# Fixed tiles of a twelve-phase transformer kernel placed at multiples of 512 bytes

## The chip, the cores and the metric

The kernel runs on 1 core of one Trainium2 chip. The metric is the device time of one execution in microseconds (us), lower being better. TensorE multiplies matrices into PSUM, VectorE (DVE) and ScalarE (ACT) do elementwise work, and the queue of SyncE (SP) issues the transfers between HBM and SBUF. SBUF has 128 partitions; an address below is the byte offset inside a partition, the same in all 128.

## The reference, cut to what matters

The input is 256 tokens of width 1024 in float32. Two blocks follow each other, each twice (depth 2). The first block is conditioned: a vector c gives shift, scale and gate for each of three steps (feed-forward, a mixer of four groups, feed-forward). The second has three steps of the same kind with plain gains and norms on both sides.

```python
for l in range(DEPTH):                       # first block
    sh1, sc1, g1, ... = split(silu(c) @ ada_w[l] + ada_b[l], 9)
    hn = modulate(rms_norm(h, g), sh1, sc1)
    h = h + 0.5 * g1 * swiglu(hn, ffn1_w_in[l], ffn1_w_out[l])      # 1024 -> 2 x 2816 -> 1024
    z = modulate(rms_norm(h, g), sh2, sc2) @ w_in[l]                # attention, convolution, gMLP, forgetting attention
    h = h + g2 * (concat(o_a, o_b, o_c, o_d) @ w_out[l])
    h = h + 0.5 * g3 * swiglu(modulate(rms_norm(h, g), sh3, sc3), ffn2_w_in[l], ffn2_w_out[l])
for l in range(DEPTH):                       # second block
    x = x + 0.5 * rms_norm(swiglu(rms_norm(x), ...))
    x = x + rms_norm(merged(hgrn2, sliding attention) @ w_out[l])
    x = x + 0.5 * rms_norm(swiglu(rms_norm(x), ...))
```

All of it is float32. The weights of the large products, 692 tiles of 512 KB in the packing of the kernel, are read once.

## The kernel before, in words

There are twelve phases, 0 to 11: three per layer, two layers per block, two blocks. Phases 0, 2, 3, 5, 6, 8, 9 and 11 are feed-forwards, phases 1 and 4 mixers of the first block, 7 and 10 of the second. By the trace of before, phase 0 ends at about 228 us, phase 2 runs from about 372 to 565, phase 3 from there to 763, the first block ends at about 1084 and phase 8 begins at about 1478.

The activations of a norm lie transposed in two fixed tiles, xh and xl, [128 features, 8 x 256 tokens]: the value rounded to the tensor engine's float32r, and the rest. A weight tile [128, 1024] is loaded raw (wr, 3 buffers), ScalarE casts it to wh (9 buffers; L321) and VectorE subtracts to get wl (9 buffers; L322). A large product is three passes, in `mm3` at L346 to L349:

```python
T.matmul(acc, a, wh, start=start, stop=False)     # L347: high part times high part
T.matmul(acc, a, wl, start=False, stop=False)     # L348
T.matmul(acc, b, wh, start=False, stop=stop)      # L349: low part
```

The first operand behind the accumulator, [128, 128], is stationary and is loaded before each pass; the second, [128, 512], moves. In the trace a product is written with the moving operand first (`a<-wh,xh`).

Two loops call it. `gemm_cols` and `gemm_pair` (a "column product") take xh and xl as stationary operands and hold two accumulators per chunk of 512 columns, one for each half of the tokens. `gemm_rows` (a "row product") takes the stationary operands from scratch slots: gh and gl of a hidden chunk, made by `split` into slots of the s2 pool (22 buffers of 2048 bytes, names s in the trace), and goes round four accumulators. The two are never mixed: a column product's stationary operand is always xh or xl, a row product's always a slot. Two small products have operands elsewhere: L1101 moves lev_h over lf, and the gate column of the first block (L347 with `t<-xh,wf`) moves xh over 4 columns of wf.

The order on each engine comes from a scheduler that follows the program's order by priority; weights are called for two keys ahead (AHEAD), and the modulation columns of the first block (ada, 144 tiles of 512 KB, L628) are loaded and multiplied on VectorE between the pieces of phases 0 to 5, spread by PACE0, PACEM and PACE1.

Where the tiles lie is set by the order in which the pools' tiles are made. The fixed tiles (pool const) come first, from byte 16512 of each partition, in the order h, col_sb, identb, xh, xl, epsc, mod, an (sizes 8192, 3520, 256, 8192, 8192, 8, 288 twice, 96 twice, each rounded up to 32). The pools wr, wh, wl, s2, s1, sm and row follow, then the pools of the blocks. So the bytes past a multiple of 512 were: h 128, xh and xl 320, every slot of wr, wh, wl and s2 96, lev_h 96, lf 480, wf 352 and 96, ada 224.

Of the kernel before, what the change touches and what calls it, by code (L numbers as in the profile page):

```python
# [9 lines left out]
F32 = mybir.dt.float32  # L10
F32R = mybir.dt.float32r
# [11 lines left out]
TAPS = 31  # L23
FIRST = 3  # chunks of the first product that share its k-outer loop
AHEAD = 2  # weight tiles loaded before their use
TAIL, TAIL1 = 4, 3  # last weight tiles of a product that run one token tile after the other
NORM_WAIT = 5  # pieces of a product between a norm's arithmetic and its transposes
CONV_STEP = 2  # taps of the convolution per piece
BOOST = 40  # instructions by which a norm's chain comes forward
PACE0, PACEM, PACE1 = 30.0, 3.0, 31.0  # weight tiles over which a phase spreads its modulation columns  # L30
NS2, NS1, NW, NR, NA = 22, 5, 9, 3, 2  # buffers

# [190 lines left out]
def body(ctx, tc, ws, cols, x, c, adaw, wf, gmn, wst, bmask, lev, pred, sbias, gains, lbs, out, phases=range(12)):  # L223
# [39 lines left out]
    def row_tile():  # L263
        return row_p.tile([128, D], F32, tag="row", name=nm("row"))

    h = const.tile([128, 2, D], F32, name="h")
    col_sb = const.tile([128, NCOL], F32, name="col_sb")
# [6 lines left out]
    identb = const.tile([128, 128], BF16, name="identb")  # L274
    xh = const.tile([128, 8, S], F32R, name="xh")
    xl = const.tile([128, 8, S], F32R, name="xl")
    epsc = const.tile([128, 2], F32, name="epsc")
# [3 lines left out]
    @contextmanager  # L281
    def sooner(n):
        """the instructions inside come before ones emitted up to n earlier where both are ready"""
        p0 = tc.cur_priority
        tc.cur_priority = p0 - n
        yield
        tc.cur_priority += n

# [1 line left out]
    threads = []  # L290
# [27 lines left out]

# [1 line left out]
    def split(dst_h, dst_l, src):  # L320
# [3 lines left out]
    loaded = {}  # L324
# [44 lines left out]
    def gemm_pair(key0, key1):  # L369
        """the first two chunks of a phase: token tile 0 of both, then token tile 1"""  # L370
        acc = [[accum(), accum()] for _ in range(2)]
        w = {}
        for t in range(2):
            until(lambda: t in normed)
            for n, key in enumerate((key0, key1)):
                if t == 0:
                    w[n] = [weights(key + (i,)) for i in range(2)]
                for k in range(8):
                    mm_cols(acc[n], w[n], k, t)
                    if k % 2:  # L380
                        pump()
        normed.clear()
        return acc
# [30 lines left out]

# [1 line left out]
    def rsqrt(dst, src, scale, eps=0):  # L416
        """1 / sqrt(scale * src + eps) from the tables, refined by a Newton step"""
        n = src.shape[1]
        v, a = sm(n), sm(n)
        A.activation(a, src, AF.Ln, scale=scale, bias=epsc[:, eps:eps + 1])  # L420
        A.activation(a, a, AF.Exp, scale=-0.5)
        V.tensor_scalar(out=v, in0=src, scalar1=scale, scalar2=(1.0, 4.0)[eps] * EPS, op0=ALU.mult, op1=ALU.add)
        V.tensor_tensor(out=v, in0=v, in1=a, op=ALU.mult)
        V.scalar_tensor_tensor(out=v, in0=v, scalar=-0.5, in1=a, op0=ALU.mult, op1=ALU.mult)
        V.scalar_tensor_tensor(out=dst, in0=v, scalar=1.5, in1=a, op0=ALU.add, op1=ALU.mult)
# [7 lines left out]
    def row_rstd(halves, half=False, boost=0):  # L433
        """1 / rms of rows given as two halves; half: 0.5 / rms"""
        ss = sm(2)
        for i, src in enumerate(halves):
            junk = s1([128, 512], BF16)
            A.activation(junk, src, AF.Square, accum_out=ss[:, i:i + 1])  # L438
        r = sm(1)
        with sooner(boost):  # L440
            V.tensor_tensor(out=r, in0=ss[:, 0:1], in1=ss[:, 1:2], op=ALU.add)
            rsqrt(r, r, (4.0 if half else 1.0) / D, 1 if half else 0)
        return r
# [13 lines left out]
    def deferred(ph):  # L457
        """phases whose products take rows without their 1 / rms, which then scales the results"""
        return ph >= 6 and ph % 3 != 1
# [38 lines left out]
    def boundary(ph, t, acc):  # L498
        """residual of phase ph, norm of the next one"""
        if ph < 6 and t == 0:  # L500
# [29 lines left out]

# [1 line left out]
    def ffn(ph, first=None):  # L532
# [39 lines left out]
    def to_features(src):  # L572
        """[128 tokens, 256] x 2 token tiles -> PSUM [128 features, 2, 256 tokens]"""
        ps = tp([128, 2, S])
        for t in range(2):
            for i in range(2):
                T.transpose(ps[:, i, 128 * t:128 * t + 128], src[t][:, 128 * i:128 * i + 128], ident)  # L577
        return ps
# [16 lines left out]
    def exp_rows(ps, n, nmx, sums, cols, floor=None):  # L595
        """exp(ps - row max) of n score maps into SBUF; row sums into the given columns"""
        pb = s2([128] + list(ps.shape[1:]))
        V.tensor_reduce(out=nmx, in_=ps, axis=AX.X, op=ALU.max, negate=True)
        if floor is not None:
            V.tensor_tensor(out=nmx, in0=nmx, in1=floor, op=ALU.min)  # L600
        for i in range(n):
            A.activation(pb[:, i], ps[:, i], AF.Exp, bias=nmx[:, i:i + 1], accum_out=sums[:, cols[i]:cols[i] + 1])
        return [pb[:, i] for i in range(n)]

    def keys_first(p):
        """probabilities [queries, 128 keys] of four heads, keys on partitions"""
        ps = tp([128, 4, 128])
# [5 lines left out]

# [1 line left out]
    first_block = ctx.enter_context(ExitStack())  # L615
    mod = [const.tile([128, 72], F32, name=f"mod{l}") for l in range(2)]
    an = [const.tile([128, 24], F32, name=f"an{l}") for l in range(2)]
    c1 = pool("c1", 1, first_block)
    ada_p = pool("ada", NA, first_block)
# [12 lines left out]
    def ada_finish(l, n, w):  # L632
        """bias of columns n .. n + w of one segment; scale columns also give norm_g * (1 + scale)"""
        s = slice(n, n + w)
# [32 lines left out]
    def start():  # L667
        """the first norm's modulation as its columns arrive, FIRST chunks of the first product at a time"""
        xts = [s2([128, 2, S]) for _ in range(4)]
# [72 lines left out]
    def mix1(ph):  # L742
# [13 lines left out]
        def layer_norms(srcs):  # L756
            """normalised rows of two [128 tokens, 256]"""
            mv, r, nb = sm(4), sm(2), sm(2)
# [79 lines left out]
        def qk_norms(acc, group):  # L838
            """RMS norms over groups of columns of two [128 tokens, 512]"""
            n = 512 // group  # L840
# [11 lines left out]
        def weighted(pts, v):  # L852
            """four heads' p @ v in PSUM [128 queries, 4, 64]"""
            o = tp([128, 4, 64])
# [5 lines left out]
        def diff(acc):  # L860
# [11 lines left out]
            for t in range(2):  # L872
                keys = 128 * (t + 1)
                ts = slice(128 * t, 128 * t + 128)
                sums = sm(8)
                # maps of one 32-row group of the tensor engine share a PSUM bank
                for j in range(4):
# [43 lines left out]
        def decay():  # L921
            """the running sum of -log_sigmoid(f), heads on partitions"""
            ps = tp([4, S])
# [78 lines left out]

# [1 line left out]
    def setup2():  # L1004
# [13 lines left out]
        nc.sync.dma_start(out=sb, in_=sbias.rearrange("p (a b) -> p a b", a=8))  # L1018
        # log of the softmax over the two depths: [log(1 - lb), log(lb)]
        lb = c2.tile([128, 2, 512], F32, name="lb")  # L1020
# [18 lines left out]
    def mix2(ph):  # L1039
# [20 lines left out]
        def gates(acc):  # L1060
            """log forget gates split for the tensor engine (tokens on partitions), keys (features on partitions)"""
            lb = G2["lb"]
# [27 lines left out]
        def hgrn():  # L1090
            lf, kT, qT, v, sg = got["lf"], got["k"], got["q"], got["hv"], got["sg"]
            far, sts = [], []
            for t in range(2):
# [14 lines left out]
                def weigh(b):  # L1108
                    """decays times keys on the first half of each pair of blocks, times queries on the second"""
                    for c_, src in ((0, kT[t]), (1, qT[t])):  # L1110
# [23 lines left out]
                def second(b):  # L1134
                    """columns of the second half of each pair of blocks"""
                    return lambda ap: ap.rearrange("p h (n c b) -> p h n c b", c=2, b=b)[:, :, :, 1]
# [64 lines left out]
        def swa_kv():  # L1201
            """one 256-column chunk: keys, features on partitions, and values"""
            w = weights(("b2", l, "akv"))
# [122 lines left out]

# [1 line left out]
    rest = {0: [2, 4, 3, 5, 7, 6], 2: [8, 10, 9], 3: [11, 13, 12, 14, 16, 15], 5: [17]}  # L1328
# [79 lines left out]
```

## Time and profile before

| | |
|---|---|
| median of 3 runs | 2254.09 us |
| lowest and highest | 2253.39 and 2263.06 us |
| span of the profiled execution | 2261.4 us |
| TensorE busy, granted clock | 2185.8 us (97%), 0.990 of 2.4 GHz |
| VectorE, ScalarE busy | 1493.7 us (66%), 1188.8 us (53%) |
| read from HBM | 450.03 MB, 199 GB/s over the span |
| weight tiles | 692 transfers of 512 KB, 4.1 us from issue to landing |

The profile is one execution, and its span is 7 us over the median of the runs. The span is from the first to the last instruction of the program; the runs' times also hold what lies around it, which the profile does not show. Busy shares of TensorE count overlapping instructions once, so 97% says that it hardly pauses and not how quickly it goes.

### The profile page before, as it was taken

To read this page: it belongs to the slowest core of one execution; us is meant where nothing else is said; L and a number is where in the kernel's file an instruction comes from. 1 tells how busy PE (TensorE), PEld (TensorE's weight loads), DVE (VectorE), ACT (ScalarE), POOL (GpSimd) and SP (SyncE) were. 2 spreads that over 40 slices of the span, in tenths; PEclk is the share of its full clock that TensorE was granted. 3 is DMA by queue.
4 is the path that set the end of the run, shared out by engine and by line. 5 is a ranking of instruction groups with operands and counts; after the bars stand their busy time and mean duration, and the time that the engine had idled before them with its cause. 6 is when DMAs were issued, how large, how long until landed. Compare 5 with 4: busy or idle time off the path is not lost.

```text
span 2261.4 us, 27880 instructions
## 1 busy us (share of the span) xinstructions
PE 2185.8 (97%) x10148; PEld 1766.1 (78%) x10150; DVE 1493.7 (66%) x2251; ACT 1188.8 (53%) x1914; POOL 0.2 (0%) x4
## 2 busy tenths in 40 slices
PE   5999897999999998999999999999999999999998
PEld 4877676888788776888788888878888887887887
DVE  7878885765887786654755666575565557657553
ACT  5544655544544656543654566464455447546542
POOL 0000000000000000000000000000000000000000
PEclk9999998999999999999999999999999999999999
DMA  8889633876798733665655543475556556245652
GB/s 314 305 299 323 232 104 123 286 256 216 282 322 304 240 112 112 223 200 190 220 195 184 171 159 104 139 220 184 184 180 200 183 167 199 92 142 165 203 181 93
DMA packets 125417, 452.91 MB, mean 200 GB/s; under 512 B 14176, under 2 KB 14432, under 8 KB 125280
## 3 DMA queue, kind: packets, MB, share of 16 engines
q1 hardware_dynamic: 125280, 451.13, 59.9%
q8 instruction: 80, 1.31, 0.2%
q14 instruction: 57, 0.47, 0.1%
HBM read 450.03 MB, written 1.05 MB: 199 GB/s over the span
## 4 chain that ended last, share of the span: by engine, by line
PE 73%; DMA 11%; DVE 7%; ACT 5%; issue 3%; SPq 0%; DVEq 0%; ACTq 0%
PE a L347 22%; PE a L349 21%; PE a L348 21%; DMA wr<-in_ws 9%; DVE wl L322 3%; ACT wh L321 3%; PE t L577 2%; DVE spill L628 1%; DMA ada<-in_adaw 1%; PE t L451 1%; PE t L1147 1%; PE t L1101 1%; PE t L883 1%; ACT h L438 1%; PE t L609 0%
## 5 line engine op out<-in xcount | busy, mean ns | idle before, releaser
L322 DVE TENSOR_TENSOR wl<-wr,wh 128x1024 fp32r<-128x1024 f32 x692 | 844.2, 1223 | 493.2 <-ACT wh L321 490.7
L321 ACT CAST wh<-wr 128x1024 fp32r<-128x1024 f32 x692 | 725.7, 1051 | 753.4 <-PE a L349 430.4
L347 PE MATMUL a<-wh,xh 128*128 128x512 f32 x1888 | 761.5, 404 | 20.9 <-ACT xh L686 8.3
L348 PE MATMUL a<-wl,xh 128*128 128x512 f32 x1888 | 746.9, 396 | 0.0
L349 PE MATMUL a<-wh,xl 128*128 128x512 f32 x1888 | 745.7, 396 | 0.0
L347 PEld LDWEIGHTS a<-wh,xh 128*128 128x128 f32 x1888 | 357.7, 190 | 106.6 <-ACT xh L686 10.5
L349 PEld LDWEIGHTS a<-wh,xl 128*128 128x128 f32 x1888 | 356.3, 189 | 88.5 <-DVE xl L496 2.2
L348 PEld LDWEIGHTS a<-wl,xh 128*128 128x128 f32 x1888 | 357.8, 190 | 79.3
L347 PE MATMUL a<-wh,s 128*128 128x512 f32 x896 | 352.8, 394 | 7.8 <-ACT s L321 3.9
L348 PE MATMUL a<-wl,s 128*128 128x512 f32 x896 | 351.6, 392 | 1.7 <-DVE wl L322 1.7
L349 PE MATMUL a<-wh,s 128*128 128x512 f32 x896 | 349.9, 392 | 0.3 <-DVE s L592 0.3
L347 PEld LDWEIGHTS a<-wh,s 128*128 128x128 f32 x896 | 168.8, 188 | 45.0 <-ACT s L321 5.1
L348 PEld LDWEIGHTS a<-wl,s 128*128 128x128 f32 x896 | 169.0, 189 | 36.9 <-DVE wl L322 2.8
L349 PEld LDWEIGHTS a<-wh,s 128*128 128x128 f32 x896 | 169.1, 189 | 36.1 <-DVE s L592 0.7
L628 DVE CUSTOM_DVE_ANT_0 spill<-ada,cond 128x1024 bf16<-128x1024 f32 x144 | 175.6, 1220 | 17.3 <-DMA ada<-in_adaw 16.3
L451 PE MATMUL t<-col_sb,s 128*128 128x128 f32 x304 | 46.8, 291 | 31.9 <-DVE s L474 26.3
L451 PEld LDWEIGHTS t<-col_sb,s 128*128 128x128 f32 x304 | 36.8, 148 | 45.0 <-DVE s L474 18.9
L322 DVE TENSOR_TENSOR s<-t,s 128x512 fp32r<-128x512 f32 x96 | 64.7, 683 | 1.9 <-ACT s L321 1.7
L321 ACT CAST s<-t 128x512 fp32r<-128x512 f32 x96 | 54.9, 583 | 18.6 <-PE t L577 18.6
L577 PE MATMUL t<-col_sb,h 128*128 128x128 f32 x392 | 58.3, 273 | 3.7 <-DVE h L546 2.1
L542 ACT ACTIVATE h<-a,m 128x256 f32<-128x256 f32 x88 | 40.6, 472 | 39.5 <-PE a L349 39.4
L577 PEld LDWEIGHTS t<-col_sb,h 128*128 128x128 f32 x392 | 47.8, 140 | 17.2 <-DVE h L546 3.3
(234 smaller groups left out, 1249.6 us busy)
## 6 DMA issues: line engine op xcount, KB each, us to landing
wr<-in_ws SPq DMA_DIRECT2D x692, 512.0 KB, 4.1
ada<-in_adaw SPq DMA_DIRECT2D x144, 512.0 KB, 4.8
row<-in_gains SPq DMA_DIRECT2D x12, 512.0 KB, 4.9
h<-in_x SPq DMA_DIRECT2D x2, 512.0 KB, 5.7
out<-h SPq DMA_DIRECT2D x4, 256.0 KB, 2.1
cond<-in_c SPq DMA_DIRECT2D x1, 512.0 KB, 4.2
gmn<-in_gmn SPq DMA_DIRECT2D x2, 256.0 KB, 5.3
wst<-in_wst SPq DMA_DIRECT2D x2, 256.0 KB, 6.1
```

The costliest lines, as they stand in the source:

```text
L321: A.copy(dst_h, src)
L322: V.tensor_tensor(out=dst_l, in0=src, in1=dst_h.bitcast(F32), op=ALU.subtract)
L347: T.matmul(acc, a, wh, start=start, stop=False)
L348: T.matmul(acc, a, wl, start=False, stop=False)
L349: T.matmul(acc, b, wh, start=False, stop=stop)
L438: A.activation(junk, src, AF.Square, accum_out=ss[:, i:i + 1])
L451: T.transpose(ps[:, j], src[:, 128 * j:128 * j + 128], ident)
L542: A.activation(g, acc[t][:, 0:256], AF.Silu, scale=r)
L577: T.transpose(ps[:, i, 128 * t:128 * t + 128], src[t][:, 128 * i:128 * i + 128], ident)
L628: ins = V.tensor_tensor_reduce(out=spill, in0=raw, in1=cond, scale=1.0, scalar=0.0, op0=ALU.mult, op1=ALU.add, accum_out=mod[l][:, n:n + 1])
L883: T.matmul(ps[:, i], qT[rs, i, ts], kT[rs, i, 0:keys], start=False, stop=i == 1)
L1101: T.matmul(ps.rearrange("p a b -> p (a b)"), lf[t][n][:, hs], G2["lev"][:, o:o + 512], start=n == 0, stop=n == 1)
```

## The change

The fixed tiles are made in another order: an unused tile of 384 bytes, xh, xl, h, col_sb, identb, epsc, mod, an, and an unused tile of 32 bytes. The first moves xh to byte 16896 (33 x 512), the last moves the first weight buffer to byte 46080 (90 x 512). As the slots are 4096 and 2048 bytes long, the bytes past a multiple of 512 become: h, xh and xl 0, every slot of wr, wh, wl and s2 0, lev_h 0, lf 384, wf 256 and 0, ada 128. The instructions, their order on each engine and what each waits for are those of before. The diff also drops comments and docstrings.

```diff
+    const.tile([128, 96], F32, name="lead")
+    xh = const.tile([128, 8, S], F32R, name="xh")
+    xl = const.tile([128, 8, S], F32R, name="xl")
     h = const.tile([128, 2, D], F32, name="h")
     col_sb = const.tile([128, NCOL], F32, name="col_sb")
...
     ident = C("ident")
     identb = const.tile([128, 128], BF16, name="identb")
-    xh = const.tile([128, 8, S], F32R, name="xh")
-    xl = const.tile([128, 8, S], F32R, name="xl")
     epsc = const.tile([128, 2], F32, name="epsc")
...
     mod = [const.tile([128, 72], F32, name=f"mod{l}") for l in range(2)]
     an = [const.tile([128, 24], F32, name=f"an{l}") for l in range(2)]
+    const.tile([128, 8], F32, name="trail")
     c1 = pool("c1", 1, first_block)
```

## Rows read from the trace of the kernel before

**Rows 1.** Page: busy us, share of the span; DMA share and GB/s in 40 slices.

```profile
PE 2185.8 (97%) x10148; PEld 1766.1 (78%) x10150; DVE 1493.7 (66%) x2251; ACT 1188.8 (53%) x1914; POOL 0.2 (0%) x4
...
DMA  8889633876798733665655543475556556245652
GB/s 314 305 299 323 232 104 123 286 256 216 282 322 304 240 112 112 223 200 190 220 195 184 171 159 104 139 220 184 184 180 200 183 167 199 92 142 165 203 181 93
```

**Rows 2.** Page: shares of the chain that ended last, by line.

```profile
PE a L347 22%; PE a L349 21%; PE a L348 21%; DMA wr<-in_ws 9%; DVE wl L322 3%; ACT wh L321 3%; PE t L577 2%; DVE spill L628 1%; DMA ada<-in_adaw 1%; PE t L451 1%; PE t L1147 1%; PE t L1101 1%; PE t L883 1%; ACT h L438 1%; PE t L609 0%
```

**Rows 3.** Chain by line: stretches 0-252, 252-567, 567-768, 768-2262 us, in this order.

```profile
by line: DMA wr<-in_ws 40.8%; issue 9.0%; ACT wh L321 8.8%; DVE spill L628 8.6%; DVE wl L322 8.6%; DMA ada<-in_adaw 5.8%; DMA col_sb<-in_cols 2.7%; PE a L347 2.1%; PE a L348 2.0%; PE a L349 2.0%; DVE s L322 1.2%; SPq L627 0.8%; DVE s L474 0
by line: PE a L349 23.7%; PE a L347 23.7%; PE a L348 23.5%; issue 3.2%; DVE wl L322 2.4%; PE t L883 2.2%; DMA wst<-in_wst 2.1%; PE t L857 1.7%; PE t L451 1.6%; PE t L577 1.5%; DMA wr<-in_ws 1.4%; PE t L964 1.3%; PE t L962 1.3%; ACT wh L321 
by line: DMA wr<-in_ws 20.7%; PE a L347 15.9%; PE a L349 15.9%; PE a L348 15.7%; DMA ada<-in_adaw 7.1%; ACT wh L321 5.0%; issue 4.6%; DVE wl L322 3.8%; DVE spill L628 3.8%; PE t L577 1.5%; ACT s L494 0.9%; DVE h L546 0.9%; PE t L451 0.8%; A
by line: PE a L347 25.1%; PE a L349 24.9%; PE a L348 24.9%; DMA wr<-in_ws 3.9%; PE t L577 1.9%; DVE wl L322 1.7%; ACT wh L321 1.6%; issue 1.4%; PE t L1147 1.2%; PE t L451 1.2%; PE t L1101 1.0%; ACT h L438 0.8%; PE t L1259 0.7%; PE t L1241 0
```

**Rows 4.** Busy time by stretch, in us; last three: granted clock, DMA share, GB/s.

```profile
core 0: us, PE busy (x) PEld busy (x) DVE busy (x) ACT busy (x) POOL busy (x), PEclk, DMA share, GB/s
567.00:768.00 201.00, 195.92 (x871) 157.76 (x870) 163.27 (x235) 98.72 (x141) 0.00 (x0) 0.99 0.84 298
1465.00:2262.00 797.00, 783.79 (x3672) 638.68 (x3670) 469.31 (x638) 419.63 (x656) 0.00 (x0) 1.00 0.53 170
1109.00:1115.00 6.00, 6.00 (x28) 4.81 (x27) 4.07 (x4) 2.88 (x5) 0.00 (x0) 1.00 0.81 268
1229.00:1236.00 7.00, 7.00 (x33) 5.79 (x32) 3.27 (x3) 2.81 (x3) 0.00 (x0) 1.00 0.63 205
```

**Rows 5.** Timeline of TensorE, product from xh, xl: start us, us, instruction; 22 rows.

```profile
1109.70 0.40 PE L349 MATMUL a<-wh,xl 128*128 128x512 f32 x1
...
1114.60 0.39 PE L349 MATMUL a<-wh,xl 128*128 128x512 f32 x1
```

**Rows 6.** Timeline of TensorE, product from scratch slots; 27 rows.

```profile
1229.81 0.39 PE L347 MATMUL a<-wh,s 128*128 128x512 f32 x1
...
1235.70 0.39 PE L349 MATMUL a<-wh,s 128*128 128x512 f32 x1
```

**Rows 7.** Timeline of TensorE, L1101 behind a product.

```profile
1325.13 0.39 PE L349 MATMUL a<-wh,xl 128*128 128x512 f32 x1
1325.36 2.02 PE L1101 MATMUL t<-lev_h,lf 128*128 128x512 f32 x8
```

**Rows 8.** Timeline of TensorE, the product with wf; 8 rows.

```profile
804.36 0.28 PE L347 MATMUL t<-xh,wf 128*4 128x256 f32 x1
...
805.15 0.28 PE L348 MATMUL t<-xl,wf 128*4 128x256 f32 x1
```

**Rows 9.** Groups by shape, TensorE: count, busy us, mean ns, idle before.

```profile
L347 PE MATMUL a<-wh,xh 128*128 128x512 f32 x1856 | 752.2, 406 | 20.9 <-ACT xh L686 8.3 <-ACT xh L495 7.5 <-ACT wh L321 3.0
L347 PE MATMUL a<-wh,s 128*128 128x512 f32 x896 | 352.8, 394 | 7.8 <-ACT s L321 3.9 <-ACT wh L321 3.0 <-ACT s L591 0.7
```

**Rows 10.** Timeline of TensorE, a bf16 product and what follows.

```profile
1375.03 0.38 PE L1237 MATMUL t<-sb,identb 128*128 128x512 bf16 x1
1375.24 1.05 PE L1241 MATMUL t<-h,s 128*128 128x128 f32 x8
```

**Rows 11.** Groups by shape, ScalarE and VectorE.

```profile
L321 ACT CAST s<-t 128x512 fp32r<-128x512 f32 x96 | 54.9, 583 | 18.6 <-PE t L577 18.6
L321 ACT CAST xh<-t 128x512 fp32r<-128x512 f32 x24 | 13.8, 579 | 1.0 <-PE t L451 0.7
L322 DVE TENSOR_TENSOR s<-t,s 128x512 fp32r<-128x512 f32 x96 | 64.7, 683 | 1.9 <-ACT s L321 1.7
L322 DVE TENSOR_TENSOR xl<-t,xh 128x512 fp32r<-128x512 f32 x24 | 16.1, 686 | 5.7 <-ACT xh L321 5.5
```

## The prediction

> **What bounds the kernel now.** I read the page's busy table and slices first, then the chain of waits, then both stage by stage. TensorE is busy 97% of the span, VectorE 66%, ScalarE 53% [rows 1], and the three lines of the three-pass product (L347 to L349) hold 64% of the chain [rows 2]. The stages differ. From 768 us to the end those lines hold 75% of the chain and weight transfers 4%; from 252 to 567 us it is 71% and 1.4%. From 0 to 252 us they hold 6%: the chain runs through the weight transfer, its cast, its subtraction and the modulation columns. From 567 to 768 us it is mixed, 48% products and 28% transfers [rows 3], with the queue at 298 GB/s, against 170 GB/s later [rows 4]. So a shorter product counts in all stages but phases 0 and 3.
>
> A busy TensorE may still run at different paces, and the timeline of its starts shows that it does. The durations overlap and are of no use here; the starts are. In a product from xh and xl, 22 rows from 1109.70 to 1114.60 us are 21 steps: 4.90 / 21 = 0.2333 us each [rows 5]. In a product from scratch slots, 27 rows from 1229.81 to 1235.70 us are 26 steps: 5.89 / 26 = 0.2265 us [rows 6]. Same shape, same granted clock (1.00, the 2.4 GHz level) [rows 4], same number of weight loads, no wait on either side: 6.8 ns differ.
>
> What differs is where the stationary operand lies. The moving weights (wh, wl) begin 96 bytes past a multiple of 512 in both. Scratch slots also begin at 96, xh and xl at 320. A third pair: the gates' sums (L1101) move lev_h (96) over lf (480); the eight begin at 1325.36 us and their busy stretch is 2.02 us, so with 0.39 us for the last one the seven steps are 0.233 us [rows 7]. Equal remainders go with the quick pace, unequal ones with the slow one, in another line with another operand. A fourth pair is less clear: eight 256-column products of the gate column move xh (320) over wf (352 and 96) with only 4 columns to load; 0.79 / 7 = 0.113 us, or 0.226 us for 512 columns, the quick pace [rows 8].
>
> The Trainium skill ("TensorE: Matmul & The Clock Gate", Step-by-step: what each phase is for) says that TensorE has two independent read ports and that loading the next stationary tile takes no read bandwidth from the running matmul. By that, the remainders would cost nothing and the two paces would have some other cause; the rows don't decide it, so this is the first rival below.
>
> **The change part by part.** No instruction is added, removed, reordered or given another wait; only addresses move.
>
> *xh, xl and weight slots to a common remainder.* After the change the stationary xh and xl, the scratch slots and the weights all begin at 0 past a multiple of 512, so every large product has equal remainders, as scratch-slot products have now. I take the quick pace for all: 0.2333 - 0.2265, rounded to 6.7 ns saved per product. There are 3 x 1856 = 5568 such products of 512 columns [rows 9]. By the code: 528 in each of 8 feed-forward phases (11 chunks x 8 k x 2 token tiles x 3 passes), 240 in each mixer of the first block, 432 in each mixer of the second. Where products lead the chain:
> - Feed-forward phases 2, 5, 6, 8, 9 and 11: 6 x 528 x 6.7 ns = 21.2 us.
> - Second block's mixers: 2 x 432 x 6.7 ns = 5.8 us.
> - First block's mixers: 2 x 240 x 6.7 ns = 3.2 us, of which I take half, since much of them is small attention work.
> - Phases 0 and 3: 7.1 us by count, taken as nothing. A quicker product there only waits for the next weights. Some of phase 3's half could stay, so up to 3 us more.
>
> The sum is 28.6 us. In the later stages some 7% of the chain is transfer, cast and subtraction [rows 3]; where a slot is late a quicker TensorE waits longer. Taking 6% off leaves 27 us. No other engine becomes the bound: from 1465 us on VectorE is busy 469 of 797 us, ScalarE 420, and the queue would rise from 170 to about 173 GB/s [rows 4].
>
> *Scratch slots and weights to remainder 0.* Their remainders were equal and stay equal, 96 becoming 0. I take no change, from [rows 6]. Bounds: if 0 were a bad place, the slow pace of [rows 5], +6.8 ns; if the quick pace too holds a penalty of place that goes, the nearest row is a 512-column bf16 product followed after 0.21 us (1375.03 to 1375.24) [rows 10]. That operand has half the bytes, so I keep it as an end only.
>
> *ScalarE and VectorE operands.* A cast of 512 from PSUM takes 583 ns into a scratch slot (96) and 579 ns into xh (320); the subtraction 683 and 686 ns [rows 11]. Under 1% between places; value 0. Both engines have cover wherever TensorE leads; in the first 252 us, where casts and subtractions are 17% of the chain [rows 3], 1% of that is 0.4 us.
>
> *DMA destinations.* Weight tiles go from 96 to 0, modulation tiles from 224 to 128. The trace has no destination at 0, so I bound it by the slices: the first, which also fills h and col_sb at 128, moves 314 GB/s, the next two 305 and 299 [rows 1]. A spread of 4% over the 200-odd us in which transfers lead phases 0 and 3 is 8 us either way; I take 0, because the difference between those slices is also one of demand. The Trainium skill ("DMA: Bandwidth & Descriptors", How a descriptor splits into AXI transactions) says that a transaction which reads must start at a multiple of 256 bytes. Carried over to the side that is written, a 4096-byte row placed at 96 takes 17 transactions and at 0 takes 16, an estimate of at most 6% in transfers and some 12 us in those two phases; no row here shows such a step.
>
> *The two unused tiles* (384 and 32 bytes) are never read or written: 0.
>
> The profiled execution spans 2261.4 us, 7 us over the median of 2254.1 and near the slowest run (2263.06); the sum would put a span like it at 2234. From the median: 2254.1 - 27 = 2227, which I forecast, with 2217 to 2238 as this case's own range (8 us of transfers and half of phase 3's share one way; 8 us of transfers and some more late slots the other).
>
> **The rivals.**
> *The place decides nothing* (chance 0.22). The two paces belong to the two loops: column products alternate two accumulators and have transposes between them, row products go round four. For it: place and loop are tied together in [rows 5] and [rows 6], and the 4-column case is quick with unequal remainders. Against it: L1101 is neither loop and has the slow pace. Time: 2254, within 2246 to 2262.
>
> *Remainder 0 is a bad place* (0.16). It would be the stationary operand's own place that counts, and 96 happens to be a good one; xh at 320 is at a multiple of 64 as 0 is, the scratch slots are not; but lf at 480 is not either, and it is slow. Then the scratch-slot products lose 6.8 ns and xh keeps its pace. Of 3 x 896 = 2688 [rows 9], 528 are in phases 0 and 3; 2160 x 6.7 ns = 14.5 us, so 2268. It decides as soon as the row products step by more than 0.230 us. If both kinds became one step slower still, 6432 x 6.7 ns = 43 us more; I give that almost nothing.
>
> *Both paces shorten* (0.12). None of these products has a moving operand at a multiple of 128, so the quick pace may itself carry a penalty. At 0.215 us, the product from xh saves 18.3 ns on 4272 products outside phases 0 and 3 (78 us) and the others 11.5 ns on 2160 (25 us). With a tenth lost to late slots that is 93 us: 2161.
>
> **How the numbers follow.** The forecast has 0.50. The range must leave out at most 2 in 10: from 2185, which leaves out most of the last rival (0.10), to 2270, which takes in the nothing-happens case and half of the slow one (0.08 left out). Runs of this kernel spread by 0.4%, so within 0.5% (11 us, 2243 to 2265) is what can't be told from no change. Faster: 0.48 of the forecast, 0.12 of the last rival and 0.02 of the first, 0.62. Same: 0.19 of the first, 0.02 of the forecast, 0.03 of the second, 0.24. Slower: 0.13 of the second and 0.01 of the first, 0.14.
>
> **What would show it.** In the changed kernel's timeline, the starts of a column product (L347 to L349 from xh, xl) step by 0.2265 us: that is the forecast. The row products stay at 0.2265. L1101 moves lev_h at 0 over lf at 384, still unequal, and should stay at 0.233. The stretch led by transfers at the start should shrink by no more than 3 us. The forecast is wrong if the column product still steps by 0.233 (first rival), if the row product steps by over 0.230 (second), or if either goes clearly under 0.224 (third). If the steps shrink and the span does not, the time has gone to weight transfers: the chain after 768 us would then hold well over 4% of them.

## The result, and the profile after

The changed kernel takes 2237.46 us (median of 4 runs, 2233.64 to 2240.41), beside 2256.19 us for the kernel before on the same occasions (4 runs, 2253.39 to 2263.06). The ratio is 0.9894 with a 95% interval of 0.9870 to 0.9917: 1.1% faster, clear of the 0.5% that can be told apart. The two medians taken by themselves differ by 18.7 us, or 0.8%, which is the far end of that interval. The span of the profiled execution fell by 25.5 us, from 2261.4 to 2235.9; the profile of before is that of its slowest run (2263.06 us), so this difference is larger than that of the runs. All 43 runs of the kernel before that are on record, those beside the experiments included, have a mean of 2257.8 us, and the ten of the changed kernel one of 2236.6: 21 us, give or take 3.

The page of the changed kernel, busy times and slices; then the chain by line. A line number after is one higher than before in the large product (L348 to L350).

```profile
PE 2158.2 (97%) x10150; PEld 1769.1 (79%) x10150; DVE 1494.1 (67%) x2251; ACT 1188.7 (53%) x1914; POOL 0.2 (0%) x4
...
DMA  8898633876788733665665543465556556245652
GB/s 314 312 319 308 237 104 127 292 263 212 284 318 310 241 118 113 224 202 195 220 202 187 170 161 99 147 218 194 185 178 207 186 170 198 90 146 167 206 183 94
```

```profile
PE a L348 21%; PE a L350 21%; PE a L349 21%; DMA wr<-in_ws 10%; ACT wh L322 3%; DVE wl L323 3%; PE t L578 2%; DVE spill L630 1%; DMA ada<-in_adaw 1%; PE t L452 1%; PE t L1149 1%; PE t L1103 1%; PE t L885 1%; PE t L859 0%; PE t L1261 0%
```

Against [rows 1] and [rows 2]: VectorE's busy time is the same to 0.1% (1494 us) and the rate of the queue is up by no more than the shorter span asks for. TensorE is busy 28 us less and still 97% of the span. Over the whole span no other engine has taken over; TensorE goes through the same work more quickly.

The step itself, from the timeline of TensorE's starts: a column product (22 rows, 21 steps), then a row product (22 rows).

```profile
1005.35 0.40 PE L349 MATMUL a<-wl,xh 128*128 128x512 f32 x1
...
1010.12 0.39 PE L349 MATMUL a<-wl,xh 128*128 128x512 f32 x1
```

```profile
1010.57 0.39 PE L348 MATMUL a<-wh,s 128*128 128x512 f32 x1
...
1015.33 0.39 PE L348 MATMUL a<-wh,s 128*128 128x512 f32 x1
```

4.77 / 21 = 0.227 us where [rows 5] had 0.2333, and 4.76 / 21 = 0.2267 as in [rows 6]. Over all steps under 0.240 us the column product went from 233.3 to 227.4 ns and the row product stayed at 227.1. L1103 (L1101 before), whose lf is at 384 beside lev_h at 0, kept its eight in 2.02 us, as in [rows 7]:

```profile
1311.75 2.02 PE L1103 MATMUL t<-lev_h,lf 128*128 128x512 f32 x8
```

The chain of the changed kernel in the stretches 0 to 252, 567 to 768 and 768 us to the end, which answer to [rows 3]:

```profile
by line: DMA wr<-in_ws 28.6%; PE a L348 10.2%; PE a L349 9.5%; PE a L350 9.5%; DVE spill L630 7.0%; issue 6.9%; ACT wh L322 6.6%; DMA ada<-in_adaw 5.6%; DVE wl L323 4.7%; DMA col_sb<-in_cols 2.7%; PE t L578 1.2%; DVE s L475 0.9%; ACT s L495
by line: DMA wr<-in_ws 40.4%; ACT wh L322 8.8%; DVE wl L323 8.3%; DMA ada<-in_adaw 8.3%; issue 7.0%; DVE spill L630 6.4%; PE a L349 4.8%; PE a L350 4.6%; PE a L348 4.6%; PE t L452 1.2%; SPq L629 1.0%; DVE s L323 1.0%; ACT s L495 0.9%; DVE h
by line: PE a L348 24.9%; PE a L350 24.8%; PE a L349 24.7%; DMA wr<-in_ws 3.8%; PE t L578 2.0%; ACT wh L322 1.6%; issue 1.6%; DVE wl L323 1.6%; PE t L452 1.4%; PE t L1149 1.2%; PE t L1103 1.0%; PE t L1261 0.7%; PE t L1243 0.7%; DVE h L516 0
```

After 768 us products hold 74% and weight transfers 3.8%, as before. From 567 to 768 us it is 14% products and 49% transfers, where it was 48 and 28. It would be easy to read this as products that have become quicker than the transfers can follow, but the shares do not show it. Up to 252 us they moved the other way, products from 6% to 29%. And a kernel whose column products keep the 0.233 us, the third experiment below, whose phase 3 begins within 3 us of where it began before, has the same chain from 567 to 768 us:

```profile
by line: DMA wr<-in_ws 41.0%; DMA ada<-in_adaw 10.2%; ACT wh L323 8.8%; DVE wl L324 8.5%; issue 7.8%; DVE spill L630 6.5%; PE a L349 3.3%; PE a L350 3.1%; PE a L351 2.9%; PE t L453 1.2%; DVE h L548 1.2%; ACT s L496 0.9%; SPq L629 0.8%; ACT 
```

Up to 252 us the products' share lies between 6% and 38% in the profiles of all kernels with all transfers, whatever their pace. So in these two stretches the chain's shares swing from profile to profile and say nothing of the change. What limits the gain there is asked by an experiment below.

### The profile page after: what moved, and what is told of

The parts are those of the page before. It is cut to its first block, busy times and chain, and to the rows that moved or that the text cites. A ratio compares the mean times of both kernels' runs of the same rounds, so it can differ in the third digit from the quotient of the medians.

```text
span 2235.9 us, 27882 instructions
## 1 busy us (share of the span) xinstructions
PE 2158.2 (97%) x10150; PEld 1769.1 (79%) x10150; DVE 1494.1 (67%) x2251; ACT 1188.7 (53%) x1914; POOL 0.2 (0%) x4
## 4 chain that ended last, share of the span: by engine, by line
PE 73%; DMA 12%; DVE 7%; ACT 5%; issue 3%; SPq 0%; DVEq 0%; ACTq 0%
PE a L348 21%; PE a L350 21%; PE a L349 21%; DMA wr<-in_ws 10%; ACT wh L322 3%; DVE wl L323 3%; PE t L578 2%; DVE spill L630 1%; DMA ada<-in_adaw 1%; PE t L452 1%; PE t L1149 1%; PE t L1103 1%; PE t L885 1%; PE t L859 0%; PE t L1261 0%
## 5 line engine op out<-in xcount | busy, mean ns | idle before, releaser
L323 DVE TENSOR_TENSOR wl<-wr,wh 128x1024 fp32r<-128x1024 f32 x692 | 844.5, 1224 | 475.9 <-ACT wh L322 471.1
L322 ACT CAST wh<-wr 128x1024 fp32r<-128x1024 f32 x692 | 726.8, 1052 | 739.9 <-PE a L350 406.9
L348 PE MATMUL a<-wh,xh 128*128 128x512 f32 x1888 | 752.6, 399 | 20.7 <-ACT xh L688 9.4
L349 PE MATMUL a<-wl,xh 128*128 128x512 f32 x1888 | 737.5, 391 | 0.0
L350 PE MATMUL a<-wh,xl 128*128 128x512 f32 x1888 | 737.4, 391 | 0.0
L348 PEld LDWEIGHTS a<-wh,xh 128*128 128x128 f32 x1888 | 358.0, 190 | 95.8 <-ACT xh L688 11.5
L350 PEld LDWEIGHTS a<-wh,xl 128*128 128x128 f32 x1888 | 357.1, 189 | 78.0 <-DVE xl L497 1.7
L348 PE MATMUL a<-wh,s 128*128 128x512 f32 x896 | 353.5, 395 | 9.9 <-ACT wh L322 5.2
L350 PE MATMUL a<-wh,s 128*128 128x512 f32 x896 | 350.3, 392 | 0.3 <-DVE s L593 0.3
L348 PEld LDWEIGHTS a<-wh,s 128*128 128x128 f32 x896 | 169.3, 189 | 47.7 <-ACT wh L322 6.9
L350 PEld LDWEIGHTS a<-wh,s 128*128 128x128 f32 x896 | 169.4, 189 | 35.9 <-DVE s L593 0.7
L452 PE MATMUL t<-col_sb,s 128*128 128x128 f32 x304 | 46.1, 288 | 35.3 <-DVE s L475 25.7
L452 PEld LDWEIGHTS t<-col_sb,s 128*128 128x128 f32 x304 | 36.1, 147 | 48.6 <-DVE s L475 19.3
L603 ACT ACTIVATE s<-t,m 128x128 f32<-128x128 f32 (+1 forms) x80 | 32.9, 418 | 52.4 <-DVE m L601 26.6
```

Of the source, the lines that this page charges most:

```text
L322: A.copy(dst_h, src)
L323: V.tensor_tensor(out=dst_l, in0=src, in1=dst_h.bitcast(F32), op=ALU.subtract)
L452: T.transpose(ps[:, j], src[:, 128 * j:128 * j + 128], ident)
```

## The experiments

Eleven kernels follow, the last of them the changed kernel once more. "Past" below means bytes past a multiple of 512.

**Equality without alignment.** The kernel before, with xh and xl at 96 like its weights and slots, and all else in place:

```diff
+    const.tile([128, 72], F32, name="lead_a")
     xh = const.tile([128, 8, S], F32R, name="xh")
     xl = const.tile([128, 8, S], F32R, name="xl")
+    const.tile([128, 56], F32, name="lead_c")
```

> The kernel before with xh and xl moved from 320 to 96 bytes past a multiple of 512; weights and scratch slots stay at 96, h, lf, wf and ada stay where they were. Theory (equal remainders of moving and stationary operand make the quick pace): column products step by 0.227 us as in the changed kernel, time 2232 to 2243 us, ratio to before 0.988 to 0.993. Rival (it is the multiple of 512, or of 64, that helps): column products keep 0.233 us and the time stays within 0.3% of before.

Measured: 2237.56 us against 2258.18, ratio 0.9902 (0.9882 to 0.9922), the whole gain of the change. The column product in its timeline, 22 rows:

```profile
1000.20 0.39 PE L349 MATMUL a<-wh,xh 128*128 128x512 f32 x1
...
1004.96 0.39 PE L349 MATMUL a<-wh,xh 128*128 128x512 f32 x1
```

4.76 / 21 = 0.2267 us with no tile of the product at a multiple of 512, or even of 64. So it is not the multiples of 512 that give the gain; equal places are enough.

**Inequality in the other loop.** The changed kernel with the scratch slots moved by 224:

```diff
+    pool("pa").tile([128, 56], F32, name="pa_t")
     s2_p = pool("s2", NS2)
+    pool("pb").tile([128, 72], F32, name="pb_t")
```

> The changed kernel with the scratch slots alone moved from 0 to 224; weights, xh and xl stay at 0. Theory (equal remainders): row products, whose stationary operand is a scratch slot, slow from 0.227 to 0.233 us a step, 2688 of them, and the time rises by 10 to 15 us over the changed kernel, to 2247 to 2252 us; column products stay at 0.227. Rival (the loop decides, or xh and xl had a bad place of their own): row products stay at 0.227 and the time at 2237 us.

Measured: 2248.55 us, ratio to before 0.9955 (0.9940 to 0.9970), so 11 us of the gain are gone, as expected. Row products, 22 rows:

```profile
1010.70 0.39 PE L350 MATMUL a<-wh,s 128*128 128x512 f32 x1
...
1015.60 0.40 PE L350 MATMUL a<-wh,s 128*128 128x512 f32 x1
```

4.90 / 21 = 0.2333 us, the pace that column products had, now in the other loop, while column products stay at 0.227. The same loop has now run at both paces with nothing but the places changed, so the loop and its accumulators do not make the difference, and the rival "the place decides nothing" falls.

**A multiple of 512 under the stationary operand alone.** The kernel before with xh and xl at 0 and everything else at 96 (192 bytes ahead of xh, 320 behind xl):

```diff
+    const.tile([128, 48], F32, name="lead_a")
     xh = const.tile([128, 8, S], F32R, name="xh")
     xl = const.tile([128, 8, S], F32R, name="xl")
+    const.tile([128, 80], F32, name="lead_c")
```

> The kernel before with xh and xl moved from 320 to 0; weights and scratch slots stay at 96. Theory (equal remainders): unequal as before, 96 apart in place of 224, so column products keep about 0.233 us a step and the time stays near before, 2250 to 2260 us. Rival (a multiple of 512 under the stationary operand is what counts): 0.227 us and 2237 us.

Measured: 2264.0 us in its one run, a little over what was expected, against 2252 to 2266 for the kernel before on the same occasion. Column product, 22 rows:

```profile
1005.57 0.39 PE L350 MATMUL a<-wl,xh 128*128 128x512 f32 x1
...
1010.47 0.39 PE L350 MATMUL a<-wl,xh 128*128 128x512 f32 x1
```

4.90 / 21 = 0.2333 us: no gain, so a multiple of 512 under the stationary operand by itself is worth nothing.

**Which distance counts.** The changed kernel with xh and xl at other places (the pads ahead of and between them changed):

```diff
-    const.tile([128, 96], F32, name="lead")
+    const.tile([128, 160], F32, name="lead_a")
     xh = const.tile([128, 8, S], F32R, name="xh")
+    const.tile([128, 96], F32, name="lead_b")
     xl = const.tile([128, 8, S], F32R, name="xl")
+    const.tile([128, 96], F32, name="lead_c")
```

> The changed kernel with xh at 256 and xl at 128 past a multiple of 512, everything else at 0 as there. If equality is wanted modulo 512, all three passes of a column product are slow, 0.233 us. If modulo 256, the steps beside which xh is loaded (before L348's pass and before the next product) stay at 0.227 and the one beside which xl is loaded slows. If modulo 128, all stay at 0.227; the slow pace of lf at 384 over lev_h at 0 speaks against that.

Measured: 2249.6 us in one run. 22 rows of the column product, all three passes mixed, are 4.86 / 21 = 0.231 us:

```profile
1000.13 0.40 PE L352 MATMUL a<-wh,xl 128*128 128x512 f32 x1
...
1004.99 0.40 PE L352 MATMUL a<-wh,xl 128*128 128x512 f32 x1
```

By pass, over all starts: 228.1 ns where xh at 256 is loaded beside wh, 232.2 where xl at 128 is loaded beside wl, and 233.5 in the pass behind that, in which xl is in use and xh is loaded. So 256 apart is as good as 0 and 128 is not, as modulo 256 has it; that the pass behind is slow too was not expected. A pass's step is here the time from its start to the next start.

**Small distances.** The same with xh at 64 and xl at 32:

```diff
+    const.tile([128, 112], F32, name="lead_a")
     xh = const.tile([128, 8, S], F32R, name="xh")
+    const.tile([128, 120], F32, name="lead_b")
     xl = const.tile([128, 8, S], F32R, name="xl")
+    const.tile([128, 120], F32, name="lead_c")
```

> The changed kernel with xh at 64 and xl at 32 past a multiple of 512, everything else at 0 as there. The two pairs of before the runs so far leave two readings. If only equality modulo 256 is quick, all three passes of a column product step by 0.231 to 0.234 us, the row products by 0.227, and the time is near 2252 us. If a step smaller than 128 bytes is harmless (the operand is still in the same piece of memory), they stay at 0.227 and the time at 2237 us.

Measured: 2269.9 us in one run; 235.3 to 236.0 ns in two passes, 232.2 in the third:

```profile
1000.11 0.40 PE L351 MATMUL a<-wl,xh 128*128 128x512 f32 x1
...
1005.06 0.40 PE L351 MATMUL a<-wl,xh 128*128 128x512 f32 x1
```

4.95 / 21 = 0.2357 us, slower than the kernel before and than the 0.231 to 0.234 us and 2252 us that were expected. A small distance is no better than a large one.

**Places mixed, equal modulo 256.** The changed kernel with xh, xl and the tiles beside them at 0 or 256 past, and lf where lev_h is, modulo 256 (xh and xl by pads of 160, 64 and 128 elements in the same places):

```diff
+    pool("pw").tile([128, 64], F32, name="pw_t")
     wl_p = pool("wl", NW)
...
+        pool("pl").tile([128, 96], F32, name="pl_t")
         lf_p = pool("lf", 4)
```

> The changed kernel with its places mixed over multiples of 256: xh, wl, scratch slots and lev_h at 256, xl, wh and lf at 0. If equality modulo 256 is all that counts, column and row products step by 0.227 us, L1101 goes from 0.231 to 0.227, and the time is that of the changed kernel, 2232 to 2243 us. If equality modulo 512 is wanted, the passes that mix 0 and 256 slow and the time rises to 2250 us or more.

Measured: 2234.68 us, ratio 0.9908 (0.9884 to 0.9933), the changed kernel's time. Column product, 22 rows, and the first eight of the gates' sums, where lf is now as lev_h modulo 256:

```profile
1000.14 0.39 PE L351 MATMUL a<-wh,xh 128*128 128x512 f32 x1
...
1004.90 0.39 PE L351 MATMUL a<-wh,xh 128*128 128x512 f32 x1
```

```profile
1311.40 1.99 PE L1106 MATMUL t<-lev_h,lf 128*128 128x512 f32 x8
```

0.2267 us; and (1.99 - 0.39) / 7 = 0.229 us in place of 0.233 for these eight sums. Over all 52 steps of such sums the mean went from 232.2 to 229.7 ns, half of the way to the 227 expected. For the large products equality modulo 256 is enough.

**Which operand the pace goes by.** The changed kernel with wl alone at 128:

```diff
+    pool("pw").tile([128, 32], F32, name="pw_t")
     wl_p = pool("wl", NW)
+    pool("pv").tile([128, 96], F32, name="pv_t")
```

> The changed kernel with wl alone moved from 0 to 128; xh, xl, wh and scratch slots stay at 0. It asks which operand the pace goes by. If a step is slow when its moving operand and the operand loaded beside it differ modulo 256, only L349's pass (the one that moves wl) slows, to 0.232 us, in column and row products alike, and the others stay at 0.227. If what counts is a change of place from one load to the next, as when xl alone lay at 128, nothing slows, since all stationary operands lie at 0. If the slow pace carries over into the next step, L350's pass slows too.

Measured: 2263.6 us in one run. Column product, then row product, 22 rows each:

```profile
1001.29 0.39 PE L351 MATMUL a<-wl,xh 128*128 128x512 f32 x1
...
1006.18 0.40 PE L351 MATMUL a<-wl,xh 128*128 128x512 f32 x1
```

```profile
1018.23 0.40 PE L350 MATMUL a<-wh,s 128*128 128x512 f32 x1
...
1023.09 0.39 PE L350 MATMUL a<-wh,s 128*128 128x512 f32 x1
```

4.89 / 21 = 0.233 and 4.86 / 21 = 0.231 us. By pass it is 233.2, 232.0 and 231.1 ns: all three slow, although only one moves an operand at another place. Row products have 234.2, 232.7 and 230.7 ns. None of the three expected readings is right. One unequal operand makes other passes slow as well, one more when it was the loaded operand xl, both others when it was the moving operand wl. In a round of three passes, what comes behind an unequal pass also comes ahead of the next one, so these runs cannot say which way it carries over; that stays open, and so does why the first pass is the slowest here.

**Where the gain is lost: transfers.** Both kernels with the modulation weights loaded once, so that phases 0 to 5 move 75 MB less. The first block's modulation is then not the reference's, and VectorE no longer waits for these tiles:

```diff
-        raw = ada_p.tile([128, D], F32, tag="ada", name=nm("ada"))
-        nc.sync.dma_start(out=raw, in_=adaw[l, n])
+        if "raw" not in rows:
+            rows["raw"] = ada_p.tile([128, D], F32, tag="ada", name=nm("ada"))
+            nc.sync.dma_start(out=rows["raw"], in_=adaw[l, n])
+        raw = rows["raw"]
```

> The kernel before with the modulation weights loaded once instead of 144 times (every one of the 144 products on VectorE reads the first tile, so the first block's modulation is not the reference's); 75 MB less in phases 0 to 5. It is one half of a pair with the next run. Theory (in phases 0 and 3 transfers take back what the products gain): without these transfers phases 0 and 3 shorten by 10 us or more together, and this kernel takes 2225 to 2245 us.

> The changed kernel with the same edit as the run before this (modulation weights loaded once; the first block's modulation is not the reference's). Theory (transfers take the gain back in phases 0 and 3): the change is now worth more, 28 to 32 us between the two kernels in place of some 25, with 2.5 us or more of it in each of phases 0 and 3. Rival (the gain is lost in these phases to something else, such as slots of the weights): still 23 to 26 us, and phases 0 and 3 gain under 1 us each.

Measured: 2246.25 us (before, ratio 0.9951, 0.9936 to 0.9966) and 2217.54 us (changed, 0.9836, 0.9807 to 0.9864). The first is just above the 2245 us expected at most; phases 0 and 3 of the kernel before are 17 us shorter together. The change is now worth 28.7 us by the medians, 26 by the two ratios and 33.1 by the two spans (2248.3 and 2215.2), where with all transfers the medians differ by 18.7 and 21.9 us on two occasions. By the runs' means the two gains, 28 and 21 us, differ by 7 us with an uncertainty of nearly as much, so the times of the phases must carry the argument. The stretches of phases 0 and 3 of the changed kernel, first as it is, then with one load of modulation weights:

```profile
0.00:227.00 227.00, 198.37 (x860) 160.12 (x860) 181.25 (x307) 107.80 (x154) 0.20 (x4) 0.98 0.88 314
557.00:755.00 198.00, 191.28 (x862) 156.38 (x861) 161.10 (x230) 94.53 (x135) 0.00 (x0) 0.99 0.85 302
```

```profile
0.00:215.00 215.00, 193.50 (x858) 158.48 (x859) 178.85 (x312) 109.04 (x156) 0.20 (x4) 0.99 0.57 193
545.00:735.00 190.00, 188.22 (x863) 155.45 (x862) 158.22 (x231) 96.64 (x137) 0.00 (x0) 1.00 0.55 183
```

The queue falls from 314 and 302 GB/s to 193 and 183, and without its load the products' pace shows: from the first product to the last, phase 0 takes 196.3 us in the one kernel and 193.2 in the other, phase 3 192.6 and 189.6, 3.0 us each. In the chain of phase 3 products now hold 95% in both, and no transfer is among its first nine entries; before and after the change, in this order:

```profile
by line: PE a L347 31.8%; PE a L349 31.7%; PE a L348 31.7%; PE t L577 2.5%; ACT s L494 1.0%; PE t L451 0.8%; PE t L660 0.5%; ACT xh L495 0.3%; issue 0.0%
by line: PE a L348 31.8%; PE a L349 31.7%; PE a L350 31.5%; PE t L578 2.5%; ACT s L495 1.0%; PE t L452 0.8%; PE t L662 0.5%; ACT xh L496 0.3%; issue 0.0%
```

With all transfers the profiles of five kernels with column products at 0.231 us or more (before and four experiments) have phase 3 at 198.0 to 199.2 us, and six profiles with 0.227 us have 196.7 to 201.0: no difference that the scatter would let through. So in phase 3 it is the transfers that take the gain; for phase 0 the same rests on one pair of profiles.

**Where the gain is lost: the second block's mixers.** In phases 7 and 10 the changed kernel's TensorE waits before the transposes of the gates' keys, L452, 2.4 us each time for ScalarE's exponent at L1082. The view lists TensorE's waits of phase 7, from 1260 to 1463 us:

```profile
PE t L452 <- ACT s L1082: 2.4, 1, 2.4
PE t L452 <- DVE s L477: 0.5, 1, 0.5
PE t L452 <- DVE m L442: 0.2, 1, 0.2
```

Before, that wait was 0.8 us in phase 7; in phase 10 it was 1.4 us, with another 1.2 us before the gates' sums. The exponent does not come sooner with quicker products: in phase 7 it ends 41.4 to 43.0 us after the first column product in the profiles of either pace. In phase 10 of the changed kernel's profile something else adds to it, which the waits do not list. TensorE's granted clock was at the lower of its two levels (1.2 GHz, share 0.50) for 3.4 us shortly after the wait, and products step by 0.43 us there:

```profile
1882.71 0.66 PE L452 MATMUL t<-col_sb,s 128*128 128x128 f32 x4 [2.39 <-ACT s L1082]
...
1884.13 0.63 PE L350 MATMUL a<-wh,xl 128*128 128x512 f32 x1
...
1887.54 0.40 PE L349 MATMUL a<-wl,xh 128*128 128x512 f32 x1
```

```profile
1884.10:1887.50 3.40, 3.40 (x9) 2.67 (x8) 3.40 (x6) 3.40 (x7) 0.00 (x0) 0.50 0.00 0
```

The eight steps from 1884.13 to 1887.54 us take 3.41 us, 1.6 more than at 0.227. Before the fall TensorE had stood 2.4 us and worked for 1.4; the equal wait of phase 7 was followed by none. The profile of before has no such fall in phase 10. The fall is not tied to the change: four of the seven profiles with column products at 0.227 us have it at this place, and two of the six others. The profiles that have it do not have the 1.2 us wait before the sums. So in this pair phase 10 loses 2.4 + 1.6 us after, against 1.4 + 1.2 before.

An edit to take the wait away, one more piece of product ahead of these transposes, with 128 bytes ahead of lf:

```diff
             yield
             yield
+            yield
             got["lf"] = lf
             got["k"] = [heads_T(k) for k in ks]
...
+        pool("pl").tile([128, 32], F32, name="pl_t")
         lf_p = pool("lf", 4)
```

> The changed kernel with the gates' transposes of the second block one piece later (one more yield before them), and lf moved to 0, equal to lev_h. In the changed kernel TensorE waits there for ScalarE's exponent, 2.8 us in each of phases 7 and 10, against 1.2 and 3.4 before. Theory (the quicker products arrive sooner at a chain of fixed length): both waits go and the span is 3 to 5 us under the changed kernel's of the same call. Rival (the chain only delays what comes behind it, the products of the mixing that wait for the keys): the wait moves to another line and the span stays within 1 us.

> The changed kernel once more, on the chip of the run before this, for the comparison with it: 2232 to 2242 us, ratio to before 0.987 to 0.992, column products at 0.227 us a step.

Measured: 2237.21 us (ratio 0.9898, 0.9878 to 0.9919) and 2235.78 us for the changed kernel again (0.9904, 0.9882 to 0.9927). No gain. TensorE's waits with the edit, from 1266 to 1470 us, and where the first of them lies:

```profile
PE t L452 <- ACT s L1082: 1.9, 1, 1.9
PE t L452 <- DVE s L477: 0.4, 1, 0.4
```

```profile
1311.12 0.60 PE L452 MATMUL t<-col_sb,s 128*128 128x128 f32 x4
1315.49 0.66 PE L452 MATMUL t<-col_sb,s 128*128 128x128 f32 x4 [1.91 <-ACT s L1082]
```

The two rows are the transposes of the two halves of the tokens, each with an exponent of its own. The first half, which had the 2.4 us, no longer waits; the second, which did not wait before, now waits 1.9 us for its exponent, which ends 5 us after the first one. So the wait has moved and not gone, as the expected rival had it, though on the same line. Behind it the granted clock was at the lower level for 3.4 us here too (from 1316.3 us), over the first of the gates' sums, so the length of phase 7 in this profile does not tell what the edit is worth without that. From the first column product of phase 7 to that of phase 8 the profiles have 201.1 us before, 200.9 after, 200.6 for it again and 201.5 with the edit. This stage's length is not set by the products alone: of the 2.5 us that 432 quicker steps give, 1.6 went into the longer wait (2.4 for 0.8). Where the rest went was not taken apart. No kernel tried that computes the same is faster than the changed one by more than the intervals.

## Why the prediction was right, point by point

**The mechanism** held as written: equal remainders, the quick pace for all large products, row products and L1101 as they were. Its first rival fell with the two kernels that moved one operand without touching the loops, the second (0 a bad place) with the row products at 0.2267 us, the third (both paces shorten) likewise. Where the prediction spoke of a multiple of 512, 256 would have been enough. How the two operands get in each other's way is not shown; the runs show only which places cost time.

The Trainium skill ("TensorE: Matmul & The Clock Gate", Step-by-step: what each phase is for) says that loading the next tile's weights takes no SBUF read bandwidth from the running matmul. By that the places of the two would cost nothing, as the first rival had it. These runs do not agree: operands 224 bytes apart cost 5.9 ns a step in column products (233.3 against 227.4) and 6.2 in row products (233.3 against 227.1). Whether it is read bandwidth that is lost, no run shows.

The Trainium skill's rule on 256-byte transactions ("DMA: Bandwidth & Descriptors", How a descriptor splits into AXI transactions), carried over to the side that is written, would have shortened transfers by the estimated 6% at most. Phase 0, which the queue leads, moved 310 GB/s before and 314 after, and weight tiles land in 4.1 us in both, so no such step shows.

**The price of a step** was 6.7 ns in the sum (the two readings differ by 6.8) and came to 5.9 (233.3 to 227.4). The rows that it was read from are clean stretches; a column product is broken by transposes, and the steps next to a break still take 0.231 to 0.232 us on average. Summed over all starts, what the column products' steps under 0.240 us take over 0.227 fell from 32.6 to 2.5 us: 30.1 us saved, where 5568 x 6.7 ns would be 37. The longer steps, in which TensorE waits or has other work between, grew by 4.6 us in both kinds of product together, and 30.1 - 4.6 is the 25.5 us by which these two spans differ.

**By stage,** from the first column product of a phase to that of the next, one profile each:

| phases | forecast | measured, us |
|---|---|---|
| 2, 5, 6, 8, 9, 11 | 21.2 | 3.0, 2.7, 3.2, 4.2, 2.6, 3.1; 18.9 together |
| 7, 10 | 5.8 | 0.2, 0.8; 1.0 together |
| 0 and 1, 3, 4 | 1.6 | 4.3, 0.4, 0.8; 5.5 together |

The feed-forwards came out at nine tenths, which is the lower price of a step (5.9 for 6.7) and leaves nothing for late slots: the 6% taken off for them was put on the wrong stage. The other mis-sized term is the one of the second block's mixers, which took every product as being on the path. There TensorE comes earlier to the exponent and waits for it, 1.6 us more in phase 7, and in phase 10 this pair has the fall of the clock. Against two profiles with the 0.233 us (before, xh and xl at 0) four with the 0.227 us (after, its repeat, all at 96, places mixed) gain 0.7 and 1.2 us in these phases, so the term is worth about 2 us and not 5.8. The 4.3 us in phases 0 and 1 are within the scatter of the transfer-led start, whose phase 0 alone lies between 204 and 210 us in the profiles of all kernels with all transfers.

So the forecast of 27 us was too large by the price of a step and by the mixers. How much too large depends on what it is set against: 23.9 us by the ratio, 21 by the means of all runs, 18.7 by the medians of the first occasion. By the means it is about a quarter, and 2237.46 us lies half a microsecond inside the case's own range of 2217 to 2238: that it fell inside is partly luck. The 25.5 us of the two profiles come nearer to the forecast because the profile of before is of its slowest run.

**Engines that were to stay** did: casts 1052 ns, subtractions 1224, as before the change to 1 ns.

## What to carry to other kernels

Read the pace of a busy TensorE from the differences of starts in the timeline and compare it between loops: two loops of the same shape that differ by some per cent have a cause that can be moved. Place the stationary and the moving operands of float32r products (128 by 128 over 512 columns, as here) equal modulo 256 bytes, all of them, since one odd operand in three slowed other passes too; it costs a pad of a few hundred bytes. Other shapes need a reading of their own. Count such a gain only where products set the end, and not where transfers or a chain on other engines do. Before reading a difference of a microsecond or two between stages of two profiles, look at the granted clock in both and at a second profile of each kernel.

## What was not expected of the hardware

The penalty does not grow with the distance. Over all starts 224 and 96 bytes give 233.3 ns, 128 bytes 231 to 234 in the passes that it slows, and 64 and 32 together 232 to 236, against 227.4 for 0 and 227.5 for 0 and 256 mixed. With 256 moving columns the order turns round: the 96 such products of the second block's narrow chunk step by 0.117 us with xh at 320 beside weights at 96, and by 0.120 us with equal places (medians; in every kernel with equal places it is 0.120, and 0.119 with xh at 0 beside weights at 96). Even the quick pace is 544 cycles of the 2.4 GHz level for 512 columns, against the 0.21 us of the bf16 product in [rows 10]; no place that was tried brought it lower.
